# One layer on one core: the first double pair of gate and up as eight plain products instead of seven combined ones

## The chip, the core and the metric

The kernel runs on one core of a Trainium2 chip. The core has TensorE (PE, with its weight loads as PEld), VectorE (DVE), ScalarE (ACT), GpSimd (POOL) and a queue for transfers (SP). The metric is the device time of one execution in microseconds (us), the median over runs. Each engine works through its own list of instructions in a fixed order; a scheduler decides that order when the program is built.

## The reference, cut to what matters

The program is one transformer layer: a mixer, a cross attention and a SwiGLU block, each with a norm ahead and a norm behind. The change lies where the cross attention ends and the SwiGLU block begins:

```
x = x + rms_norm(cross_attention, xattn_norm_post)
h = rms_norm(x, ffn_norm_pre)            # 512 tokens x 1024
g, u = split(h @ w_gate_up)              # 2 x 2816 columns
y = (silu(g) * u) @ w_down
x = x + rms_norm(y, ffn_norm_post)
```

## The kernel before, in words

**Split floats.** Every operand of a product is held as two parts, hi and lo: `split` lets ACT write hi (L167) and DVE or POOL subtract it from the source to get lo (L168). A product of two operands is three matmuls, wl with hi, wh with lo, wh with hi (L1226 to L1228 for gate and up).

**Gate and up.** The 2 x 2816 columns are worked in eleven double pairs, d = 0 to 10, each of 256 columns of gate and 256 of up. In `gate_up(d)` the tokens are two halves (0 to 255, 256 to 511) and the 1024 rows of the weight are two halves (lo, hi), so h is four blocks 11, 12, 21, 22 (token half, row half). Gate and up of one double pair would be eight products of blocks. The kernel takes seven, in Winograd's form: 11, 12, S2, S1, S3, S4, 22 in that order, where S1 = 21 + 22, S2 = S1 - 11, S3 = 11 - 21, S4 = 12 - S2 are sums of token blocks, and the weights of those products are sums too (`t1`, and sums written over `ulo`, `glo`, `ghi`). A product is 24 matmuls of 256 columns.

**Where the blocks come from.** `dense_R` ends the cross attention, one token tile of 128 after another (bk_dR). Behind each tile `ev_second2` adds to the residual and calls `prenorm`, which norms the tile, transposes it on PE (bk_pn, L254) and hands it to `Blocks.store`. For tiles 0 and 1 that writes blocks 11 and 12 (A) as hi and lo; for all four tiles ACT also copies the plain numbers to a buffer `hr` (L1167). `Blocks.sums` (tiles 2 and 3, L1172 to L1178) builds S1 to S4 and 22 from the `hr` buffers with sums on DVE and POOL, and splits each of them.

**Order.** `steps` begins d = 0 and d = 1 with their product 11, then runs d = 0, then d = 1 and so on. The weights of d = 0 are in `fraw[0]` and those of d = 1 in `fraw[1]`, both loaded early: `fraw[1]` lies on the left, where the pool `tp` of the attention was.

**Down.** Behind the last double pair, `w_down` is split and multiplied (bk_ff). Weights there come from `fw[1]`, the split gate (`gs`) from `fw[0]`, four buffers each.

Of the kernel before, what the change touches and what calls it, by code (L numbers as in the profile page):

```python
# [14 lines left out]
P = 128  # L15
# [31 lines left out]
def hybrid_layer(ctx, tc, a, out):  # L47
# [13 lines left out]
    tp = late.enter_context(tc.tile_pool(name="tp", bufs=4))  # L61
    yp = late.enter_context(tc.tile_pool(name="yp", bufs=16))
    gp = late.enter_context(tc.tile_pool(name="gp", bufs=16))
    BUFS = {"sc": 3, "tr": 2, "pv": 1, "d": 2}
# [127 lines left out]
    class Big:  # L192
# [922 lines left out]
    fraw, fw, fn, fa, fg = ([pool("fr0", 2, "right")], [pool("fw0", 4, "right")], pool("fn", 2, "right"),  # L1115
                            [pool("fa0", 2, "right")], [pool("fg0", 5, "right")])
    count = [0]

    def wpair(shape=(P, 4, 256), half=None):

        if half is None:
            half = count[0] % 2
            count[0] += 1
        return [fw[half].tile(list(shape), F32R, tag="wc", name="w" + q) for q in "hl"]
# [16 lines left out]
    class Blocks:  # L1141

        def __init__(self):
            self.c, self.raw = {}, {}

        def take(self, pool, *names):
            for n in names:
                self.c[n] = pool.tile([P, 2, 4, 256], F32R, tag="A", name="A" + n)

        def put(self, n, i, src, eng=None):  # L1150
            c = slice(128 * (i % 2), 128 * (i % 2) + 128)
            t = self.c[n]
            split(t[:, 0, :, c], t[:, 1, :, c], src, eng)

        def hi(self, n, k):
            return self.c[n][:, 0, k, :]

        def lo(self, n, k):
            return self.c[n][:, 1, k, :]
# [34 lines left out]
    fw.append(pool("fw1", 4))
    fa.append(pool("fa1", 5))
    fg.append(pool("fg1", NF // 2 - 5))
    fe, ft = pool("fe", 6), pool("ft", 1)
    A.take(fa[1], "S2", "S1", "S3", "S4", "22")
    for i in range(2, NT):
        with tc.high_priority(offset=PLAN["fprio"]):  # L1200
            A.sums(i)

    Gf = {}

    def gate_up(d):

        raw = []
        for u in range(2):
            raw.append(fraw[d % 2].tile([P, KT, 256], F32, tag="raw", name="raw"))
            nc.sync.dma_start(raw[u], kview(w_gu)[:, :, FF * u + 256 * d:FF * u + 256 * d + 256])  # L1210
        g, u = raw
        glo, ghi, ulo, uhi = g[:, 0:4], g[:, 4:8], u[:, 0:4], u[:, 4:8]

        def weights(src, eng=None, half=None):
            w = wpair(half=half)
            split(*w, src, eng)
            return w

        def product(b, w, n, start):
            wh, wl = w  # L1220
            for z in range(2):
                c = slice(128 * z, 128 * z + 128)
                o = b[:, 256 * z:256 * z + 256]
                for k in range(4):
                    st = start and z == 0 and k == 0
                    nc.tensor.matmul(o, lhsT=wl[:, k, c], rhs=A.hi(n, k), start=st, stop=False, skip_group_check=True)  # L1226
                    nc.tensor.matmul(o, lhsT=wh[:, k, c], rhs=A.lo(n, k), start=False, stop=False, skip_group_check=True)  # L1227
                    nc.tensor.matmul(o, lhsT=wh[:, k, c], rhs=A.hi(n, k), start=False, stop=k == 3, skip_group_check=True)  # L1228

        def halves(t):  # L1230
            return t.rearrange("p (z t) -> p z t", z=2)
# [18 lines left out]
        yield  # L1250
# [18 lines left out]
        yield  # L1269
# [13 lines left out]
    for g in range(NF // 2):  # L1283
        raw = fraw[1 - g // 2 % 2].tile([P, 2, D], F32, tag="raw", name="raw")
        nc.sync.dma_start(raw, wd[:, 2 * g:2 * g + 2, :])
        for q in range(2):
            k = 2 * g + q
            if k >= NF - LAST:
                t = len(tail)
                gs = fw[t // 4].tile([P, 2, 512], F32R, tag="wc", name="gs")  # L1290
                w2 = fa[t >= 2].tile([P, 2, D], F32R, tag="A", name="wd")
                hi, lo = w2[:, 0, :], w2[:, 1, :]
            else:
                gs = fw[0].tile([P, 2, 512], F32R, tag="wc", name="gs")
                hi, lo = wpair((P, D), 1)
# [50 lines left out]
```

## Time and profile before

| | |
|---|---|
| median of 3 runs | 870.31 us (869.36 to 871.18) |
| the profiled execution | 870.79 us, its span 869.0 us |
| PE busy | 821.9 us, 95% of the span |
| DVE, ACT, POOL busy | 546.9, 431.9, 342.2 us |

PE is the engine that the others feed, so what counts is where it stands still or runs at its lower clock. The 40 slices of the page show that in one place in the middle of the program, in the 24th and 25th slice (a slice is 21.7 us).

### The profile page before, as it was taken

The numbers are of one execution on the slowest core, as the hardware profiler recorded it, in microseconds if no ns is written. First come the engines' busy times: TensorE is split into PE (matmuls) and PEld (weight loads), VectorE is DVE, ScalarE is ACT, GpSimd is POOL, SyncE is SP. The second block draws the span as 40 slices with busy tenths as digits, with TensorE's granted clock in tenths as the row PEclk, the third lists the DMA queues.
The fourth block names the chain that finished last, engine by engine and source line by source line (L and its number), as shares of the span: only waits on it lengthen the run. The fifth ranks groups of instructions, "written<-read, shape, count | busy, mean of one in ns | idle before, by whom it ended". The sixth has DMA issues, their size and how long they took to land.

```text
span 869.0 us, 12630 instructions
## 1 busy us (share of the span) xinstructions
PE 821.9 (95%) x4809; PEld 703.6 (81%) x4809; DVE 546.9 (63%) x913; ACT 431.9 (50%) x848; POOL 342.2 (39%) x246
## 2 busy tenths in 40 slices
PE   5899998998999999999999868999999999999997
PEld 3787667885688978778888668999999999888885
DVE  3528688687889835743553699888888775223313
ACT  5413566667867644634543654445544444224411
POOL 3405133255537443502311474644444454432320
PEclk9999999999999999999999988999999999999999
DMA  8633331321203331242226003333333333222101
GB/s 270 210 107 114 90 84 62 127 80 49 74 2 98 122 122 49 97 146 97 97 98 194 0 25 97 98 97 97 110 119 119 111 122 103 97 97 98 49 25 72
DMA packets 68307, 85.27 MB, mean 98 GB/s; under 512 B 4400, under 2 KB 53905, under 8 KB 68246
## 3 DMA queue, kind: packets, MB, share of 16 engines
q1 hardware_dynamic: 64574, 77.97, 27.7%
q10 hardware_dynamic: 3672, 6.50, 2.1%
q8 instruction: 38, 0.62, 0.3%
q14 instruction: 23, 0.19, 0.1%
HBM read 82.34 MB, written 2.12 MB: 97 GB/s over the span
## 4 chain that ended last, share of the span: by engine, by line
PE 75%; DVE 12%; ACT 6%; DMA 2%; issue 2%; POOL 1%; SPq 1%; ACTq 0%; DVEq 0%; POOLq 0%
PE bk_X L1226 5%; PE bk_X L1227 5%; PE bk_X L1228 5%; PE bk_ff L286 5%; PE bk_ff L287 5%; PE bk_ff L288 5%; PE bk_dT L286 4%; PE bk_dT L287 4%; PE bk_dT L288 4%; PE bk_pv L922 3%; PE bk_dN L287 3%; PE bk_dN L288 3%; PE bk_dN L286 3%; PE bk_Z L1226 2%; PE bk_Z L1227 2%; PE bk_Z L1228 2%
## 5 line engine op out<-in xcount | busy, mean ns | idle before, releaser
L167 ACT ACTIVATE wh<-raw 128x1024 fp32r<-128x1024 f32 x82 | 86.6, 1057 | 111.5 <-PE bk_ff L287 46.8
L168 DVE TENSOR_TENSOR wl<-raw,wh 128x1024 fp32r<-128x1024 f32 x60 | 86.2, 1439 | 60.1 <-ACT wh L167 60.1
L168 POOL TENSOR_TENSOR wl<-raw,wh 128x1024 fp32r<-128x1024 f32 x22 | 62.8, 2854 | 106.7 <-ACT wh L167 106.7
L167 ACT ACTIVATE whi<-raw 128x1024 fp32r<-128x1024 f32 (+1 forms) x64 | 60.0, 947 | 67.7 <-PE bk_dT L286 31.9
L168 POOL TENSOR_TENSOR wlo<-raw,whi 128x1024 fp32r<-128x1024 f32 x23 | 56.1, 2439 | 93.7 <-ACT whi L167 88.4
L286 PE MATMUL bk_dT<-hTh,wlo 128*128 128x512 f32 x192 | 76.9, 401 | 1.8 <-DVE wlo L168 1.1
L288 PE MATMUL bk_dT<-hTh,whi 128*128 128x512 f32 x192 | 76.6, 399 | 0.0
L287 PE MATMUL bk_dT<-hTl,whi 128*128 128x512 f32 x192 | 76.4, 398 | 0.0
L168 POOL TENSOR_TENSOR gs<-gf,gs 128x512 fp32r<-128x512 f32 x22 | 36.0, 1640 | 66.2 <-ACT gs L167 66.2
L1226 PE MATMUL bk_Z<-AS,wl 128*128 128x256 f32 x176 | 50.6, 287 | 6.6 <-DVE wl L168 6.6
L1226 PE MATMUL bk_X<-AS,wl 128*128 128x256 f32 x176 | 50.3, 286 | 3.7 <-ACT u L1249 3.7
L1226 PE MATMUL bk_X<-A,wl 128*128 128x256 f32 x176 | 50.3, 286 | 2.4 <-ACT A L167 1.3
L168 DVE TENSOR_TENSOR wlo<-raw,whi 128x1024 fp32r<-128x1024 f32 x25 | 32.7, 1313 | 31.5 <-ACT whi L167 31.3
L1227 PE MATMUL bk_Z<-AS,wh 128*128 128x256 f32 x176 | 50.6, 288 | 0.8 <-DVE AS L168 0.8
L288 PE MATMUL bk_ff<-wh,gs 128*128 128x512 f32 x128 | 50.8, 397 | 0.0
L287 PE MATMUL bk_ff<-wl,gs 128*128 128x512 f32 x128 | 50.7, 396 | 0.0
L1227 PE MATMUL bk_X<-A,wh 128*128 128x256 f32 x176 | 50.4, 287 | 0.2 <-DVE A L168 0.2
L1228 PE MATMUL bk_Z<-AS,wh 128*128 128x256 f32 x176 | 50.3, 286 | 0.0
L1228 PE MATMUL bk_X<-A,wh 128*128 128x256 f32 x176 | 50.1, 285 | 0.0
L1227 PE MATMUL bk_X<-AS,wh 128*128 128x256 f32 x176 | 49.6, 282 | 0.2 <-DVE AS L168 0.2
L1228 PE MATMUL bk_X<-AS,wh 128*128 128x256 f32 x176 | 49.5, 281 | 0.0
L892 POOL TENSOR_SCALAR s<-s,acf 128x128 f32<-128x128 f32 (+3 forms) x32 | 36.3, 1144 | 25.6 <-PE bk_tr L907 15.9
(372 smaller groups left out, 2543.4 us busy)
## 6 DMA issues: line engine op xcount, KB each, us to landing
raw<-in_w_gate_up_dram SPq DMA_DIRECT2D x22, 1024.0 KB, 7.4
raw<-in_w_down_dram SPq DMA_DIRECT2D x11, 1024.0 KB, 4.9
raw<-in_w_xkv_dram SPq DMA_DIRECT2D x8, 1024.0 KB, 5.1
raw<-in_w_in_dram SPq DMA_DIRECT2D x7, 1024.0 KB, 6.1
raw<-in_w_out_dram SPq DMA_DIRECT2D x4, 1024.0 KB, 5.1
raw<-in_w_xq_dram SPq DMA_DIRECT2D x4, 1024.0 KB
raw<-in_w_xo_dram SPq DMA_DIRECT2D x4, 1024.0 KB, 5.0
raw<-in_w_in_dram SPq DMA_DIRECT2D x6, 512.0 KB, 4.1
```

Source lines behind the costliest of these rows:

```text
L167: nc.scalar.activation(hi, src, AF.Copy)
L168: (eng or nc.vector).tensor_tensor(lo, src, hi.bitcast(F32), op=OP.subtract)
L286: nc.tensor.matmul(o, lhsT=wl, rhs=xh, start=start, stop=False)
L287: nc.tensor.matmul(o, lhsT=wh, rhs=xl, start=False, stop=False)
L288: nc.tensor.matmul(o, lhsT=wh, rhs=xh, start=False, stop=stop)
L892: ENG[on].tensor_scalar(s[:, 0:n], s[:, 0:n], c, None, op0=OP.mult)
L922: nc.tensor.matmul(o, lhsT=v, rhs=pTs[br][q][:, j], start=(br, j, q) == mms[0], stop=(br, j, q) == mms[-1])
L1226: nc.tensor.matmul(o, lhsT=wl[:, k, c], rhs=A.hi(n, k), start=st, stop=False, skip_group_check=True)
L1227: nc.tensor.matmul(o, lhsT=wh[:, k, c], rhs=A.lo(n, k), start=False, stop=False, skip_group_check=True)
L1228: nc.tensor.matmul(o, lhsT=wh[:, k, c], rhs=A.hi(n, k), start=False, stop=k == 3, skip_group_check=True)
```

## The change

- Double pair 0 is computed plainly, ahead of all sums: for each token half t, gate is 11 and 12 (or 21 and 22) with the weights' two row halves, added up in one bank, and up likewise in another. That is eight products, and neither sums of tokens nor of weights are needed for it.
- Its four weights (`w_first`) are loaded and split ahead of `dense_R` in the code.
- `store` writes all four blocks 11, 12, 21, 22 as hi and lo straight from the transposes; the `hr` copies are gone. Block 21 lies in four buffers of the pool `fe`, which moves to the right.
- `sums` comes behind the plain double pair, and gets its plain numbers back by adding hi and lo (`whole`: blocks 11 and 12 on POOL, 21 and 22 on DVE). All other sums and all their lo parts are on DVE now.
- The pool `tp` moves to the right side. `fraw[1]` now lies where the cross attention's input Ox was. `fw` is one ring of eight buffers, also for `w_down` and `gs`.
- The interleaved start of d = 0 and d = 1 is gone; d = 1 to 10 run as before, one behind the other.

```diff
+    fw = pool("fw", 8, "right")
+    fa = [pool("fa0", 3, "right")]
+    fe = pool("fe", 6, "right")
...
         def store(self, g, c0, c1, src):
             i = c0 // 128
-            if g == 0:
-                self.raw[i] = gtile(0, (P, 2, 4, 128), name="hr")
-            if i < 2:
-                self.put("12" if g else "11", i, src)
-            nc.scalar.activation(self.raw[i][:, g], src, AF.Copy)
+            self.put("%d%d" % (i // 2 + 1, g + 1), i, src)
...
         def sums(self, i):
...
+            q, r, s = (gtile((P, 2, 4, 128), name=n) for n in ("aq", "ar", "as"))
+            for n in range(2):
+                self.whole(q[:, n], "1%d" % (n + 1), i, nc.gpsimd)
+                self.whole(r[:, n], "2%d" % (n + 1), i, nc.vector)
+            nc.vector.tensor_tensor(s[:, 0], r[:, 0], r[:, 1], op=OP.add)
+            nc.vector.tensor_tensor(s[:, 1], s[:, 0], q[:, 0], op=OP.subtract)
+            self.put("S2", i, s[:, 1])
+            self.put("S1", i, s[:, 0])
+            nc.vector.tensor_tensor(r[:, 0], q[:, 0], r[:, 0], op=OP.subtract)
+            self.put("S3", i, r[:, 0])
+            nc.vector.tensor_tensor(q[:, 1], q[:, 1], s[:, 1], op=OP.subtract)
             self.put("S4", i, q[:, 1])
-            self.put("22", i, r[:, 1], nc.gpsimd)
...
+    w_first = [weights(q) for q in load_gu(0)]
...
-    for i in range(2, NT):
-        with tc.high_priority(offset=PLAN["fprio"]):
-            A.sums(i)
...
-    steps = [gate_up(d) for d in range(NF // 2)]
-    for d in (0, 0, 1, 1):
-        next(steps[d])
-    for t in steps:
-        run(t)
+    Gf[0] = gtile()
+    for t in range(2):
+        gate, up = bank("sc", "bk_X"), bank("d", "bk_Y")
+        for b, w in ((gate, w_first[0:2]), (up, w_first[2:4])):
+            for h in range(2):
+                product(b, w[h], "%d%d" % (t + 1, h + 1), h == 0, h == 1)
+        s1 = etile(name="s1")
+        nc.scalar.activation(s1, gate, AF.Silu)
+        nc.vector.tensor_tensor(Gf[0][:, :, 256 * t:256 * t + 256], halves(s1), halves(up), op=OP.mult)
+    for i in range(2, NT):
+        A.sums(i)
+    for d in range(1, NF // 2):
+        gate_up(d)
```

**ACT, where dense_R ends.** The first rows are of before, from the statistics of the last tile (pn) on; wh are hi parts of weights (raw), A11 and A12 the token blocks, xn the norm.

```order
L259 ACTIVATE pn_5025,ss1_5026<-bk_dR_4999 128x512
L167 ACTIVATE wh_5189<-raw_5183 128x1024
L167 ACTIVATE A11_4811<-bk_pn_4920 128x4x128
L247 ACTIVATE xn_4976<-x1_3426,rs_r_4980 128x512 x2
L167 ACTIVATE A12_4812<-bk_pn_4931 128x4x128
L167 ACTIVATE wh_5219<-raw_5183 128x1024
L242 ACTIVATE xn_5036,ss_5035<-x1_3426 128x1024
```

The same place after the change:

```order
L258 ACTIVATE pn_5048,ss1_5049<-bk_dR_5022 128x512
L166 ACTIVATE A11_4812<-bk_pn_4943 128x4x128
L246 ACTIVATE xn_4996<-x1_3426,rs_r_5000 128x512 x2
L166 ACTIVATE A12_4813<-bk_pn_4952 128x4x128
L241 ACTIVATE xn_5059,ss_5058<-x1_3426 128x1024
```

The two splits of weights of d = 1 are gone from between the blocks; the four of d = 0 all stand ahead of the first tile's pn.

**DVE, the sums.** Before, the sums and their lo parts (AS) begin right behind the last norm, mixed with weights (wl) of d = 0:

```order
L1172 TENSOR_TENSOR s1_5083<-hr_4989 128x512
L1173 TENSOR_TENSOR s2_5084<-s1_5083,hr_4862 128x512
L1172 TENSOR_TENSOR s1_5099<-hr_5048 128x512
L168 TENSOR_TENSOR AS2_5078<-s2_5084,AS2_5078 128x4x128
L1173 TENSOR_TENSOR s2_5100<-s1_5099,hr_4925 128x512
L168 TENSOR_TENSOR AS1_5079<-s1_5083,AS1_5079 128x4x128
L168 TENSOR_TENSOR wl_5285<-t1_5155,wh_5284 128x1024
```

After the change 27 instructions stand from the first output of the plain pair (gf, ahead of the sums) to the weight of d = 1's product S2 (wl_5415); these are the last ten of them, the second output among them:

```order
L167 TENSOR_TENSOR AS3_5099<-ar_5305,AS3_5099 128x4x128
L1257 TENSOR_TENSOR raw_5344<-raw_5345,raw_5344 128x1024
L167 TENSOR_TENSOR AS1_5098<-as_5326,AS1_5098 128x4x128
L1199 TENSOR_TENSOR aq_5324<-aq_5324,as_5326 128x512
L167 TENSOR_TENSOR AS4_5100<-aq_5304,AS4_5100 128x4x128
L167 TENSOR_TENSOR AS2_5097<-as_5326,AS2_5097 128x4x128
L1288 TENSOR_TENSOR gf_5101<-s1_5301,bk_Y_5204 128x2x256
L167 TENSOR_TENSOR AS3_5099<-ar_5325,AS3_5099 128x4x128
L1268 TENSOR_TENSOR raw_5344<-raw_5344 128x1024
L167 TENSOR_TENSOR wl_5415<-raw_5344,wh_5414 128x1024
```

The second half of S2 and the weight that goes with it now stand at the end of this chain, behind parts of S1, S3 and S4.

**SP, the loads of gate and up.** After the change (raw_4819 and raw_4820 are d = 0, raw_5344 and raw_5345 d = 1, raw_5567 and raw_5568 d = 2):

```order
L1221 DMA raw_4819<-in_w_gate_up_dram 128x8x256
L1221 DMA raw_4820<-in_w_gate_up_dram 128x8x256
L1221 DMA raw_5567<-in_w_gate_up_dram 128x8x256
L1221 DMA raw_5568<-in_w_gate_up_dram 128x8x256
L1221 DMA raw_5344<-in_w_gate_up_dram 128x8x256
L1221 DMA raw_5345<-in_w_gate_up_dram 128x8x256
```

The loads of d = 2 have moved ahead of those of d = 1, which now wait for PE's last use of Ox.

## Rows read from the trace of the kernel before

**Rows 1.** Busy time by stage; clock granted to PE, share of DMA, GB/s last
```profile
494.80:500.40 5.60, 1.81 (x10) 0.98 (x7) 4.85 (x6) 5.60 (x10) 4.25 (x5) 0.99 0.00 0
500.40:503.60 3.20, 3.08 (x14) 3.08 (x15) 3.20 (x5) 1.23 (x3) 3.20 (x2) 0.50 0.00 0
...
515.00:521.60 6.60, 0.05 (x1) 0.00 (x0) 6.60 (x6) 5.14 (x9) 5.97 (x4) 0.68 0.00 0
...
523.20:528.00 4.80, 4.74 (x23) 4.71 (x23) 4.80 (x5) 2.69 (x4) 4.61 (x3) 0.54 0.00 0
```

**Rows 2.** PE's waits from 494 to 735 us: total, times, longest
```profile
PE bk_Z L1226 <- DVE wl L168: 6.6, 1, 6.6
```

**Rows 3.** Timeline of PE: start, us, then what; in brackets the idle time before
```profile
494.43 1.03 PE L254 MATMUL bk_pn<-cc,xn 128*128 128x128 f32 x8
496.80 0.39 PE L1226 MATMUL bk_X<-A,wl 128*128 128x256 f32 x1 [1.34 <-ACT A L167]
...
505.96 0.60 PE L254 MATMUL bk_pn<-cc,xn 128*128 128x128 f32 x4
506.32 0.36 PE L1227 MATMUL bk_Y<-A,wh 128*128 128x256 f32 x1
...
521.67 0.55 PE L1226 MATMUL bk_Z<-AS,wl 128*128 128x256 f32 x1 [6.62 <-DVE wl L168]
...
523.64 0.41 PE L1228 MATMUL bk_Z<-AS,wh 128*128 128x256 f32 x1
523.85 0.41 PE L1226 MATMUL bk_Z<-AS,wl 128*128 128x256 f32 x1
...
532.89 0.35 PE L1226 MATMUL bk_X<-AS,wl 128*128 128x256 f32 x1 [1.49 <-ACT u L1249]
...
552.85 0.28 PE L1226 MATMUL bk_X<-A,wl 128*128 128x256 f32 x1
...
558.59 0.28 PE L1226 MATMUL bk_Y<-A,wl 128*128 128x256 f32 x1
```

**Rows 4.** Timeline of DVE
```profile
510.90 2.77 DVE L1173 TENSOR_TENSOR s<-s,hr 128x512 f32<-128x512 f32 x1
...
515.29 1.75 DVE L168 TENSOR_TENSOR AS<-s,AS 128x512 fp32r<-128x512 f32 x1
...
518.64 0.68 DVE L168 TENSOR_TENSOR AS<-s,AS 128x512 fp32r<-128x512 f32 x1
519.24 2.28 DVE L168 TENSOR_TENSOR wl<-t,wh 128x1024 fp32r<-128x1024 f32 x1
...
535.16 1.21 DVE L168 TENSOR_TENSOR wl<-raw,wh 128x1024 fp32r<-128x1024 f32 x1
536.30 0.67 DVE L1258 TENSOR_TENSOR p<-p,bk_X 128x512 f32<-128x512 f32 x1
...
569.64 1.23 DVE L1241 TENSOR_TENSOR raw<-raw 128x1024 f32<-128x1024 f32 x1
...
590.10 1.23 DVE L1241 TENSOR_TENSOR raw<-raw 128x1024 f32<-128x1024 f32 x1
```

**Rows 5.** Timeline of POOL
```profile
510.69 2.43 POOL L168 TENSOR_TENSOR wl<-raw,wh 128x1024 fp32r<-128x1024 f32 x1 [4.88 <-ACT wh L167]
```

**Rows 6.** Timeline of ACT
```profile
472.49 2.00 ACT L167 ACTIVATE wh<-raw 128x1024 fp32r<-128x1024 f32 x2
477.38 0.60 ACT L259 ACTIVATE pn<-bk_dR 128x512 f32<-128x512 f32 x1 [2.90 <-PE bk_dR L288]
...
494.63 0.60 ACT L259 ACTIVATE pn<-bk_dR 128x512 f32<-128x512 f32 x1
...
495.21 1.05 ACT L167 ACTIVATE wh<-raw 128x1024 fp32r<-128x1024 f32 x1
496.16 0.59 ACT L167 ACTIVATE A<-bk_pn 128x512 fp32r<-128x512 f32 x1
```

**Rows 7.** The tile raw, loads of gate and up from 440 to 560 us
```profile
DMA to landing us min/median/max: 7.6/8.1/10.0
```

More of the change, by code (lines that the diff above doesn't have):

```diff
@@ L60, in hybrid_layer @@
     sl = early.enter_context(tc.tile_pool(name="sl", bufs=6, side="right"))
-    tp = late.enter_context(tc.tile_pool(name="tp", bufs=4))
+    tp = early.enter_context(tc.tile_pool(name="tp", bufs=4, side="right"))
     yp = late.enter_context(tc.tile_pool(name="yp", bufs=16))
@@ L113, in hybrid_layer @@
         "cprio": 600,
-        "fprio": 800,
         "mprio": 100,
@@ L1114, in hybrid_layer, with wtile, weights @@
     early.close()
[L1115 to L1124, printed above, removed]
+    fraw = [pool("fr0", 2, "right")]
+    fw = pool("fw", 8, "right")
+    fn = pool("fn", 2, "right")
+    fa = [pool("fa0", 3, "right")]
+    fe = pool("fe", 6, "right")
+    def wtile(shape=(P, 4, 256), name="wc"):
+        return fw.tile(list(shape), F32R, tag="wc", name=name)
+    def weights(src, eng=None):
+        w = wtile(name="wh"), wtile(name="wl")
+        split(*w, src, eng)
+        return w
     def etile(shape=(P, 512), name="e"):
@@ L1133, in ntile, with gtile @@
         return fn.tile(shape, F32, tag="xn", name=name, bufs=2)
-    def gtile(half, shape=(P, 2, 512), name="gf"):
-        return fg[half].tile(list(shape), F32, tag="gf", name=name)
+    def gtile(shape=(P, 2, 512), name="gf"):
+        return fg.tile(list(shape), F32, tag="gf", name=name)
     class Blocks:
         def __init__(self):
-            self.c, self.raw = {}, {}
+            self.c = {}
         def take(self, pool, *names):
@@ L1148, in take, with piece, hi, lo @@
                 self.c[n] = pool.tile([P, 2, 4, 256], F32R, tag="A", name="A" + n)
+        def piece(self, n, q, k):
+            if n == "21":
+                return self.c[n][q][k // 2]
+            return self.c[n][:, q, k:k + 2, :]
+        def hi(self, n, k):
+            return self.piece(n, 0, k // 2 * 2)[:, k % 2, :]
+        def lo(self, n, k):
+            return self.piece(n, 1, k // 2 * 2)[:, k % 2, :]
         def put(self, n, i, src, eng=None):
             c = slice(128 * (i % 2), 128 * (i % 2) + 128)
-            t = self.c[n]
@@ L1153, in put @@
[L1153 to L1159, printed above, removed]
+            if n == "21":
+                for k in (0, 2):
+                    split(self.piece(n, 0, k)[:, :, c], self.piece(n, 1, k)[:, :, c], src[:, k:k + 2], eng)
+            else:
+                t = self.c[n]
+                split(t[:, 0, :, c], t[:, 1, :, c], src, eng)
         def store(self, g, c0, c1, src):
@@ new lines, in whole @@
+        def whole(self, o, n, i, eng):
+            c = slice(128 * (i % 2), 128 * (i % 2) + 128)
+            if n == "21":
+                for k in (0, 2):
+                    h, l = (self.piece(n, q, k)[:, :, c].bitcast(F32) for q in range(2))
+                    eng.tensor_tensor(o[:, k:k + 2], h, l, op=OP.add)
+            else:
+                h, l = (self.c[n][:, q, :, c].bitcast(F32) for q in range(2))
+                eng.tensor_tensor(o, h, l, op=OP.add)
+        def sums(self, i):
+            q, r, s = (gtile((P, 2, 4, 128), name=n) for n in ("aq", "ar", "as"))
[9 more added lines that the diff above has]
+            nc.vector.tensor_tensor(q[:, 1], q[:, 1], s[:, 1], op=OP.subtract)
+            self.put("S4", i, q[:, 1])
@@ new lines, in product @@
+    def product(b, w, n, start, stop=True):
+        wh, wl = w
+        for z in range(2):
+            c = slice(128 * z, 128 * z + 128)
+            o = b[:, 256 * z:256 * z + 256]
+            for k in range(4):
+                st = start and z == 0 and k == 0
+                nc.tensor.matmul(o, lhsT=wl[:, k, c], rhs=A.hi(n, k), start=st, stop=False, skip_group_check=True)
+                nc.tensor.matmul(o, lhsT=wh[:, k, c], rhs=A.lo(n, k), start=False, stop=False, skip_group_check=True)
+                nc.tensor.matmul(o, lhsT=wh[:, k, c], rhs=A.hi(n, k), start=False, stop=stop and k == 3,
+                                 skip_group_check=True)
@@ L1182, in hybrid_layer, with halves, load_gu @@
+    def halves(t):
+        return t.rearrange("p (z t) -> p z t", z=2)
+    def load_gu(d):
+        raw = [fraw[d % 2].tile([P, KT, 256], F32, tag="raw", name="raw") for _ in range(2)]
+        for u in range(2):
+            nc.sync.dma_start(raw[u], kview(w_gu)[:, :, FF * u + 256 * d:FF * u + 256 * d + 256])
+        return [raw[u][:, 4 * h:4 * h + 4] for u in range(2) for h in range(2)]
     w_gu = a["w_gate_up"][0]
@@ L1184, in hybrid_layer @@
     A = Blocks()
-    A.take(fa[0], "11", "12")
+    A.take(fa[0], "11", "12", "22")
+    A.c["21"] = [[fe.tile([P, 2, 256], F32R, tag="e", name="A21") for _ in range(2)] for _ in range(2)]
+    w_first = [weights(q) for q in load_gu(0)]
     def ev_second2(i, b):
@@ L1193, in hybrid_layer @@
     fraw.append(pool("fr1", 2))
[L1194 to L1198, printed above, removed]
-    for i in range(2, NT):
-        with tc.high_priority(offset=PLAN["fprio"]):
-            A.sums(i)
+    fa.append(pool("fa1", 4))
+    fg = pool("fg", NF // 2)
+    ft = pool("ft", 1)
+    A.take(fa[1], "S2", "S1", "S3", "S4")
     Gf = {}
     def gate_up(d):
[L1207 to L1231, printed above, removed]
+        glo, ghi, ulo, uhi = load_gu(d)
         X, Y = bank("sc", "bk_X"), bank("d", "bk_Y")
-        product(X, weights(glo, half=d if d < 2 else None), "11", True)
+        product(X, weights(glo), "11", True)
         x1 = etile(name="x1")
         nc.scalar.activation(x1, X, AF.Copy)
-        w21 = weights(ghi, nc.gpsimd, d if d < 2 else None)
+        w21 = weights(ghi, nc.gpsimd)
         t1 = ft.tile([P, 4, 256], F32, tag="t1", name="t1")
@@ L1287, in hybrid_layer @@
             k = 2 * g + q
+            gs = wtile((P, 2, 512), name="gs")
             if k >= NF - LAST:
-                t = len(tail)
-                gs = fw[t // 4].tile([P, 2, 512], F32R, tag="wc", name="gs")
-                w2 = fa[t >= 2].tile([P, 2, D], F32R, tag="A", name="wd")
+                w2 = fa[len(tail) >= 3].tile([P, 2, D], F32R, tag="A", name="wd")
                 hi, lo = w2[:, 0, :], w2[:, 1, :]
             else:
-                gs = fw[0].tile([P, 2, 512], F32R, tag="wc", name="gs")
-                hi, lo = wpair((P, D), 1)
+                hi, lo = wtile((P, D), name="whi"), wtile((P, D), name="wlo")
             split(gs[:, 0], gs[:, 1], Gf[g][:, q], nc.gpsimd)
```

18 lines of the change are left out of this document (1 added, 17 removed).

## The prediction

> **What bounds the kernel now.** I read the page first: PE is busy for 95% of the span, so the time is PE's, and a gain must come from where PE stands still or is clocked down. The windows by stage put that place right behind `dense_R` [rows 1]: from 494.8 to 500.4 PE works 1.81 of 5.6 us, then 3.2 us at a granted clock of 0.50, then it stands still from 515.0 to 521.6, and from 523.2 to 528.0 it is back at 0.54. The list of waits names the worst single one, 6.6 us, once, for a lo part of a weight on DVE [rows 2]. In those windows DVE and, mostly, POOL are busy almost without a break, so PE waits for the sums of tokens and for the weights that stand among them in DVE's order.
>
> How much that costs is read from PE's timeline [rows 3]. The last transposes that PE issues ahead of gate and up begin at 494.43 and take about 0.6 us to issue, so PE is free at about 495.05. At the other end bk_X holds the product 22 of d = 1 and then 11 of d = 2, from 552.85 to 558.59: 5.74 us for 48 matmuls, 0.1196 us each, so d = 2 begins at 552.85 + 2.87 = 555.7. Between 495.05 and 555.7 lie 60.65 us, for 14 products, or 336 matmuls, that need 40.2 us. With 16 transposes (four cost 0.36 us, from 505.96 to 506.32, so 1.44 in all) some 19 us are lost. The slow clock is in that: matmuls start 0.21 us apart at 523.64, 0.09 more than at full clock.
>
> **The change, step by step.** I lay PE's new sequence along the same time axis.
>
> Ahead of gate and up. Two more weights of d = 0 are split before the first tile's pn. ACT takes 2.00 us for two from 472.49 and waits 2.90 us before 477.38 [rows 6], so two more hide in that gap; only some 0.9 us of it is left. DVE does four lo parts instead of one, 1.13 apart, and ends just past 478; the cover is the rest of `dense_R`, 16 us of PE work. Without that cover, a late first tile would be late again at every norm behind it. I cost it at nothing.
>
> The start. Before, ACT splits a weight of d = 1 at 495.21 and only then, at 496.16, block 11 of tile 1 [rows 6], for which PE waits until 496.80 [rows 3]. In the new order that split is gone, so the block comes 0.95 earlier and PE starts at 495.85. The second matmul needs the lo part, one 0.68 subtraction [rows 4] with a handover, so PE runs from about 496.65: 1.6 us idle. A wait of 1.49 at 532.89 left the matmul at 0.35 us, not 0.55 as behind the wait of 6.62 [rows 3]; I count no clock loss here.
>
> The plain pair. Eight products, 192 matmuls at 0.1196, are 22.96, with the 1.44 of transposes: token half 0 ends at 496.65 + 11.48 + 1.44 = 509.6, token half 1 at 521.05. The extra product alone is 2.87 of it. Blocks 21 and 22 must be there at 509.6. Their lo parts read the banks of the transposes, which are issued by 507; the last of them follows by my count at about 509.3, with 0.3 us to spare for the first piece and 1.8 for the last, since its matmul comes 13 later.
>
> Double pair 1 then has 11 and 12 first (5.74, to 526.8) and needs S2 at 526.8. A whole pair in the steady part takes 590.10 - 569.64 = 20.46 us [rows 4]. With no further wait d = 1 would end at 521.05 + 20.46 = 541.5 instead of 555.7. **That is 14.2 us less, if the sums stay hidden.**
>
> The sums. DVE can begin when up of token half 0 is complete, at 509.6 and a handover, 509.9. From there to the weight of S2 stand 27 instructions: 19 of 512 elements, 4 of 256, 4 of 1024. Uncontended they follow each other at 0.60 (518.64 to 519.24) and 1.14 (535.16 to 536.30) [rows 4]; for 256 elements no row exists, between nothing and 0.60, and I take 0.35. That is 11.4 + 1.4 + 4.6 = 17.4, so 527.3: just 0.5 us late. But POOL slows DVE. While POOL runs, 512 elements take 1.75 instead of 0.68 and 1024 take 2.28 instead of 1.21, and the sum at 510.90, caught under POOL's 2.43 us from 510.69, takes 2.77 [rows 4, 5]. Two lo parts of d = 1's weights (those of ghi and of ulo) come to POOL within the chain by ACT's order, at about 517 and 528. If each holds up two instructions of DVE by 1.07, that is 4.3 us, and S2 starts at 531.6: PE waits 4.8. The Trainium skill ("SBUF — State Buffer", on the two sides of SBUF) states that the port pair which VectorE and GpSimd share is an exclusive lock for a whole instruction, so that the loser fully blocks; by that, twice 2.43 makes 4.9 instead of 4.3, and S2 0.6 later, and the 2.77 above, which ends 0.55 after POOL's instruction, agrees. A wait of this size is nearer to the 6.62 than to the 1.49, so I count the slow clock behind it: some 20 matmuls at 0.09 more (23 ran in the slow stretch from 523.2 to 528.0), 1.8. **Together 6.6 us are given back.** Bounds: 0.5 with no contention and no slow clock; 11 if the four `whole` sums on POOL (each 512 elements) also hold up DVE ahead of 509.6 by 1.07 each and so move the whole chain.
>
> What costs nothing. The `hr` copies on ACT and POOL's eight sums and splits go away (four `whole` sums come), off PE's path as soon as nothing waits for them. From S1 on the weights are back ahead of PE: after S2, DVE needs 1.14 for the next lo part and PE 2.87 per product. In `w_down` three buffers per row block come from one ring of eight, so a lo part waits for the row block two earlier; a block is 24 matmuls of twice the columns, so 2 x 2.87 = 5.7 us on PE, and the lo part 1.21 on DVE, so it is covered by some 4 us a block, and 16 blocks would pay if that cover were gone. The loads of d = 2 now start behind the first splits of weights, by my count near 476, far ahead of need. Behind SP's waiting loads of d = 1 stand only those of d = 3 and later.
>
> The sum: 870.31 - 14.2 + 6.6 = 862.7; I say 862.6. The profiled execution took 870.79, 0.48 above the median; the stage that I price lies in its span, and I subtract the difference from the median.
>
> **The rivals.**
> *The sums stay hidden* (0.20). If ACT hands POOL its weights a few instructions later or earlier, the contention falls on DVE instructions that read a bank, such as the 0.67 at 536.30, or behind the chain. Then PE waits under 2 us and the clock holds: 856 to 859. For it: POOL has far less in this stretch than before (5.97 of 6.6 us busy in the wait window). Against it: uncontended the chain is already as long as its cover.
> *The chain starts late* (0.15). The four `whole` sums on POOL meet the norm of tile 3 and two weight sums on DVE; blocks 21 and 22 come after 509.6, PE waits there, and everything behind shifts: 4 us more, 865 to 868.5.
> *Slower* (0.05). DVE's order has `t1` of d = 1 between two pieces of block 21, and it needs both loads of d = 1, which now wait for the last use of Ox. If they are issued near 491, and land 7.6 to 10.0 us later [rows 7], they are there at 501, ahead of need, which by my count of DVE's norms is at about 504. But if Ox is only released when `dense_R` has ended and the loads come behind d = 2's, each us past 506 delays blocks 21 and 22 and with them PE. From a landing at about 514 on, 8 us late with the 6.6 above, the whole 14.2 is gone; at 520 it would be 876. Nothing in the rows shows a load near twice 10 us.
> The rest of my chance (0.60) is for the forecast, 860 to 865.
>
> **How the numbers follow.** A measurement of this kernel tells about 0.2%, 1.7 us, from no change: faster means under 868.6, slower over 872. Forecast, hidden sums and nearly all of the late chain are faster: 0.92. A late chain with a further wait of 2 to 3 us would end near 870: 0.03 for the same. Slower has 0.05. The range reaches from the middle of the hidden case, 857, to the upper part of the late chain, 867; below and above lie about 2 in 10.
>
> **What would show it.** In the profile after: PE's first long row of A products from 496 to 497; no clock under 1.00 until about 527; bk_Y's product for the second token half ended at about 521; then one wait of 3 to 6 us on the first S2 matmul, for DVE's wl, and a stretch of some 4 us at about 0.50 behind it; d = 2 beginning at 548 instead of 555.7; 20.46 per pair from there, and the same span from bk_ff on. I am wrong if the wait is missing, if it lies ahead of the second token half, if DVE waits for the load of d = 1, or if PE waits in `w_down`, where it did not before.

## The result, and the profile after

The changed kernel takes 864.37 us (median of 4 runs, 862.70 to 864.66) beside 870.25 us for the kernel before on the same chip: a ratio of 0.9928, 95% interval 0.9911 to 0.9946, so 0.7% faster; the medians lie 5.9 us apart. The profiled execution took 864.1 us, its span 862.3, which is 6.7 less than the span before.

PE's waits from 485 to 735 us of the kernel after (waited for, total us, times, longest) are these; they answer to [rows 2].

```profile
engine line waited for: us in total, times, longest us
PE bk_X L1210 <- ACT u L1263: 2.4, 8, 0.6
PE bk_pn L253 <- DVE A L167: 2.0, 1, 2.0
PE bk_X L1210 <- DVE wl L167: 2.0, 1, 2.0
PE bk_Y L1210 <- POOL wl L167: 2.0, 1, 2.0
```

The one wait of 6.6 has become three of 2.0. PE's timeline has them in order of time (start, us, then the operation; in brackets the idle time ahead of it and what ended it); it answers to [rows 3].

```profile
496.63 0.39 PE L1210 MATMUL bk_X<-A,wl 128*128 128x256 f32 x1 [0.54 <-ACT A L166]
...
509.01 0.63 PE L253 MATMUL bk_pn<-cc,xn 128*128 128x128 f32 x4 [2.02 <-DVE A L167]
...
530.83 0.39 PE L1210 MATMUL bk_Y<-A,wl 128*128 128x256 f32 x1 [1.96 <-POOL wl L167]
...
535.99 0.36 PE L1210 MATMUL bk_X<-AS,wl 128*128 128x256 f32 x1 [2.01 <-DVE wl L167]
```

The windows of the same stage (columns as in [rows 1]) show the slow clock behind the first and the last of them: 0.50 from 510 to 513, 0.64 from 536 to 540.

```profile
507.00:509.00 2.00, 0.00 (x0) 0.02 (x1) 2.00 (x3) 1.97 (x4) 2.00 (x2) 1.00 0.42 136
...
510.00:513.00 3.00, 3.00 (x16) 3.00 (x15) 2.10 (x4) 1.04 (x3) 0.00 (x0) 0.50 0.00 0
...
526.00:532.00 6.00, 4.04 (x33) 3.83 (x33) 6.00 (x8) 4.07 (x5) 6.00 (x2) 1.00 0.00 0
532.00:536.00 4.00, 1.99 (x18) 1.81 (x16) 4.00 (x3) 1.06 (x1) 1.62 (x1) 1.00 0.00 0
536.00:540.00 4.00, 4.00 (x23) 4.00 (x24) 4.00 (x5) 0.63 (x1) 0.00 (x0) 0.64 0.00 0
```

What DVE did meanwhile, from its timeline after:

```profile
497.33 3.47 DVE L282 SCALAR_TENSOR_TENSOR x<-yo,rs_r,x 128x512 f32<-128x512 f32 x2
...
502.83 3.48 DVE L249 SCALAR_TENSOR_TENSOR xn<-x,rs_r,gain 128x512 f32<-128x512 f32 x2 [0.66 <-POOL rs_r L235]
506.23 0.41 DVE L167 TENSOR_TENSOR A<-bk_pn,A 128x256 fp32r<-128x256 f32 x1
506.56 1.97 DVE L1255 TENSOR_TENSOR t<-raw 128x1024 f32<-128x1024 f32 x1
508.45 1.01 DVE L167 TENSOR_TENSOR A<-bk_pn,A 128x256 fp32r<-128x256 f32 x2
...
514.51 0.69 DVE L1288 TENSOR_TENSOR gf<-s,bk_Y 128x512 f32<-128x512 f32 x1 [2.39 <-PE bk_Y L1212]
...
527.88 0.68 DVE L167 TENSOR_TENSOR AS<-as,AS 128x512 fp32r<-128x512 f32 x1
528.49 0.68 DVE L1288 TENSOR_TENSOR gf<-s,bk_Y 128x512 f32<-128x512 f32 x1
529.08 2.25 DVE L167 TENSOR_TENSOR AS<-ar,AS 128x512 fp32r<-128x512 f32 x1
531.26 3.45 DVE L1268 TENSOR_TENSOR raw<-raw 128x1024 f32<-128x1024 f32 x1
534.62 1.22 DVE L167 TENSOR_TENSOR wl<-raw,wh 128x1024 fp32r<-128x1024 f32 x1
```

And POOL's timeline:

```profile
502.76 6.90 POOL L1186 TENSOR_TENSOR aq<-A 128x512 f32<-128x512 f32 x4
521.89 11.72 POOL L167 TENSOR_TENSOR wl<-raw,wh 128x1024 fp32r<-128x1024 f32 x2 [12.23 <-ACT wh L166]
```

The two lo parts apart, from the view of the tile wl from 500 to 545 us (ns shortest/median/longest, first and last start):

```profile
L167 POOL TENSOR_TENSOR wl<-raw,wh x2: 2870/5878/8887, 521.9 to 530.7; 128x1024 fp32r<-128x1024 f32 x2
```

Read together: from 515 to 528.5 DVE is not slowed at all. Its sums start 0.60 apart and last 0.68, so the next begins before the last has ended. POOL's lo part of ghi, which needs 2.43 us [rows 5], starts at 521.89 and ends 8.89 later, at 530.78. It gets through when DVE runs an instruction that takes one input from a bank, the memory that PE writes its sums to (gf, 528.49). PE waits for that lo part until 530.83. Then DVE stands behind POOL, twice: 2.25 instead of 0.68, and 3.45 instead of 1.22. So in this chain POOL was the loser first, and PE waited for both. That isn't so in every chain of sums: in the kernel before, POOL had begun first, and then it and DVE took turns through such sums, one instruction each (512 elements in 1.75 on DVE [rows 4]; on POOL these):

```profile
513.08 1.74 POOL L1176 TENSOR_TENSOR hr<-hr 128x512 f32<-128x512 f32 x1
514.78 1.72 POOL L1178 TENSOR_TENSOR hr<-hr,s 128x512 f32<-128x512 f32 x1
```

d = 2 begins at 551.85 (bk_X holds 22 and 11 from 548.97, half of its 48 matmuls are 2.87). From PE's release at 495.68 that is 56.17 us, against 60.65 before: the stage gave 4.5 us. PE enters it 0.63 later than before (495.05). The missing 3 us lie in `w_down`. Two windows, of matmuls on bk_ff alone, first the kernel before:

```profile
760.00:830.00 70.00, 70.00 (x301) 56.26 (x300) 0.00 (x0) 0.00 (x0) 1.00 0.22 76
```

and after:

```profile
760.00:830.00 70.00, 70.00 (x310) 57.90 (x309) 0.00 (x0) 0.00 (x0) 1.00 0.21 75
```

In the same 70 us, with PE busy throughout and the full clock in both, 310 matmuls start instead of 301. Over all 528 the mean distance from one start to the next is 227.8 ns instead of 233.5, 3.0 us in all. (After the change one gap of 3.1 us is left out of this: the last 24 matmuls of gate and up run in it.) So 4.5 + 3.0 - 0.63 = 6.9, near the 6.7 of the spans.

### The profile page after: what moved, and what is told of

Its sections match the earlier page's. It is cut to its first block, busy times and chain, and to the rows that moved or that the text cites. A ratio compares the mean times of both kernels' runs of the same rounds, so it can differ in the third digit from the quotient of the medians.

```text
span 862.3 us, 12664 instructions
## 1 busy us (share of the span) xinstructions
PE 822.5 (95%) x4833; PEld 707.7 (82%) x4833; DVE 543.1 (63%) x925; ACT 424.3 (49%) x838; POOL 326.9 (38%) x238
## 5 line engine op out<-in xcount | busy, mean ns | idle before, releaser
L166 ACT ACTIVATE whi<-raw 128x1024 fp32r<-128x1024 f32 (+1 forms) x80 | 76.8, 967 | 69.6 <-PE bk_dT L285 31.9
L167 DVE TENSOR_TENSOR wlo<-raw,whi 128x1024 fp32r<-128x1024 f32 x41 | 55.0, 1343 | 80.1 <-PE bk_ff L286 43.0
L166 ACT ACTIVATE wh<-raw 128x1024 fp32r<-128x1024 f32 x64 | 67.3, 1057 | 60.6 <-PE bk_X L1210 24.5
L167 DVE TENSOR_TENSOR wl<-raw,wh 128x1024 fp32r<-128x1024 f32 x44 | 63.3, 1444 | 10.3 <-ACT wh L166 10.3
L1211 PE MATMUL bk_X<-A,wh 128*128 128x256 f32 x192 | 54.4, 283 | 0.3 <-DVE A L167 0.3
L1212 PE MATMUL bk_X<-A,wh 128*128 128x256 f32 x192 | 54.2, 283 | 0.0
L286 PE MATMUL bk_ff<-wlo,gs 128*128 128x512 f32 x128 | 49.8, 389 | 0.0
L287 PE MATMUL bk_ff<-whi,gs 128*128 128x512 f32 x128 | 49.6, 389 | 0.0
L285 PE MATMUL bk_ff<-whi,gs 128*128 128x512 f32 x128 | 47.4, 389 | 0.0
L1212 PE MATMUL bk_X<-AS,wh 128*128 128x256 f32 x160 | 45.6, 285 | 0.0
L1211 PE MATMUL bk_X<-AS,wh 128*128 128x256 f32 x160 | 45.5, 285 | 0.0
L285 PEld LDWEIGHTS bk_dT<-hTh,wlo 128*128 128x128 f32 x192 | 36.3, 189 | 10.8 <-DVE wlo L167 1.9
L1210 PE MATMUL bk_Z<-AS,wl 128*128 128x256 f32 x160 | 45.0, 281 | 0.0
```

What stands on the lines that cost most here:

```text
L166: nc.scalar.activation(hi, src, AF.Copy)
L167: (eng or nc.vector).tensor_tensor(lo, src, hi.bitcast(F32), op=OP.subtract)
L285: nc.tensor.matmul(o, lhsT=wl, rhs=xh, start=start, stop=False)
L286: nc.tensor.matmul(o, lhsT=wh, rhs=xl, start=False, stop=False)
L287: nc.tensor.matmul(o, lhsT=wh, rhs=xh, start=False, stop=stop)
```

## The experiments

The theory was: what is still lost behind `dense_R` is DVE and POOL holding each other up around the sums, and the 3 us come from where `w_down`'s buffers lie. Its rivals: the sums are simply too long for DVE, and the order of `w_down`'s products makes its pace. In the table, each ratio is to runs of the kernel before on the same chip, "stage" is worked out as from PE's first product of gate and up to the start of d = 2, and "bk_ff" is that mean distance.

| kernel | median us | ratio to before (95%) | stage us | bk_ff ns |
|---|---|---|---|---|
| before | 870.25 | | 58.9 | 233.5 |
| after the change | 864.37 | 0.9911 to 0.9946 | 55.2 | 227.8 |
| e1, no sums | 855.5 | 0.9814 to 0.9845 | 45.6 | 227.8 |
| e2, lo parts of d = 1 on DVE | 857.0 | 0.9827 to 0.9853 | 49.9 | 227.8 |
| e6, e2 and later whole sums | 856.31 | 0.9798 to 0.9842 | 47.4 | 227.8 |
| e7, later whole sums alone | 861.46 | 0.9865 to 0.9903 | 52.7 | 227.8 |
| e9, e6 and blocks moved by 32 bytes | 856.1 | 0.9781 to 0.9843 | 47.3 | 228.6 |
| e3, before with a ring in `w_down` | 869.91 | 0.9987 to 1.0005 | 59.3 | 231.9 |
| e4, before with sides swapped | 869.78 | 0.9965 to 0.9992 | 59.1 | 233.2 |
| e5, before with `fw1` on the right | 870.61 | 0.9982 to 1.0008 | 62.4 | 228.2 |
| e8, before with weights 32 bytes later | 869.78 | 0.9966 to 1.0000 | 59.6 | 231.7 |
| e10, before with sums on DVE alone | 870.5 | 0.9971 to 1.0008 | 58.0 | 233.5 |

**e1: no sums at all.**

```diff
-    A.take(fa[1], "S2", "S1", "S3", "S4")
+    A.c.update(S2=A.c["12"], S1=A.c["22"], S3=A.c["11"], S4=A.c["12"])
...
-    for i in range(2, NT):
-        A.sums(i)
```

> The changed kernel without any sums of tokens: S1 to S4 are stood in for by finished blocks, so DVE's chain and POOL's four whole sums are gone; all products and sums of weights stay. If the sums, and the two engines' contention over them, are what the plain pair still pays for, the waits on bk_Y (2.0, for POOL's wl) and on S2 (2.0, for DVE's wl) and the slow clock behind S2 (about 1.3) vanish: about 859 us, d = 2 beginning near 546.5 instead of 551.85. The wait of 2.0 on bk_pn should shrink, not vanish, since the norm of tile 3 stays: 0.5 to 2 more, so 857 to 859.5. If instead the waits come from DVE's sums of weights and splits alone, it stays at 862.5 to 864.5.

Measured 855.5 us, under the range. All three waits of 2.0 are gone, and the clock is 1.00 from 495 to 545. The first wait vanished too, which I had expected only in part. DVE's timeline says why:

```profile
503.17 1.42 DVE L249 SCALAR_TENSOR_TENSOR xn<-x,rs_r,gain 128x512 f32<-128x512 f32 x2 [0.66 <-POOL rs_r L235]
504.50 0.42 DVE L167 TENSOR_TENSOR A<-bk_pn,A 128x256 fp32r<-128x256 f32 x1
504.84 1.21 DVE L1255 TENSOR_TENSOR t<-raw 128x1024 f32<-128x1024 f32 x1
```

With no whole sums on POOL, tile 3's norm takes 1.42 instead of 3.48 and `t1` 1.21 instead of 1.97: together 2.8 us less in front of the block of tile 2 for which PE waited 2.0. So of the 55.2 us of the stage, 9.6 hang on the sums, in one way or another.

**e2: the two lo parts of d = 1 on DVE.**

```diff
-        w21 = weights(ghi, nc.gpsimd)
+        w21 = weights(ghi, nc.vector if d == 1 else nc.gpsimd)
...
-        product(X, weights(ulo, nc.gpsimd), "S3", False)
+        product(X, weights(ulo, nc.vector if d == 1 else nc.gpsimd), "S3", False)
```

> The changed kernel with the two lo parts of d = 1 that POOL makes (ghi, ulo) on DVE instead. If POOL being locked out is the cost, the wait on bk_Y (2.0) goes, DVE no longer stands behind POOL (AS at 2.25 and a sum of weights at 3.45 instead of 0.6 and 1.2, so 3.9 less, against 1.2 more for the added lo part), S2 comes some 2.7 earlier and needs no wait, and the clock holds there: 859 to 860.5 us. If the mere length of DVE's chain sets S2, the added 1.2 shows: 864.5 to 866.

Measured 857.0 us, under the range: DVE does more, and the kernel is faster still. PE's waits now:

```profile
PE bk_pn L253 <- DVE A L167: 2.0, 1, 2.0
...
PE bk_X L1210 <- DVE wl L167: 0.4, 1, 0.4
```

The waits on bk_Y and (but for 0.4) on S2 are gone. DVE runs without a break from 514.60, and the same two instructions that took 2.25 and 3.45 take:

```profile
526.17 1.22 DVE L167 TENSOR_TENSOR wl<-raw,wh 128x1024 fp32r<-128x1024 f32 x1
...
530.31 0.68 DVE L167 TENSOR_TENSOR AS<-ar,AS 128x512 fp32r<-128x512 f32 x1
530.91 1.22 DVE L167 TENSOR_TENSOR wl<-raw,wh 128x1024 fp32r<-128x1024 f32 x1
532.05 1.22 DVE L1268 TENSOR_TENSOR raw<-raw 128x1024 f32<-128x1024 f32 x1
```

The stage is 5.3 us shorter than after the change: 2.0 on bk_Y, 1.6 on S2 and some 1.2 of slow clock are 4.8 of that. The built order moved a little with the edit: an added lo part (526.17) now stands ahead of S2's weight (530.91), and the sum of weights at 532.05 behind it, so DVE has as much to do before S2 as after the change. From gf to S2 it takes 17.7 us (514.60 to 532.28) instead of 21.5 (514.51 to 535.99). So it was not the length of DVE's chain alone that PE waited for, but POOL's place in it. (The medians differ by 7.4; the spans, 862.3 and 856.4, by 5.9.)

**e6 and e7: the whole sums on POOL later,** with e2's edit and without it. The sums' target now takes the buffers of the norms xn, so that they can't begin ahead of the transposes.

```diff
-            q, r, s = (gtile((P, 2, 4, 128), name=n) for n in ("aq", "ar", "as"))
+            q = ntile((P, 2, 4, 128), name="aq")
+            r, s = (gtile((P, 2, 4, 128), name=n) for n in ("ar", "as"))
```

> As the run with d = 1's lo parts on DVE (857.0), and POOL's four whole sums take the buffers of the norms xn of tiles 2 and 3, so that they can't begin ahead of the transposes of those tiles (some 505.5 and 507 to 510 instead of 502.9). If POOL's whole sums beside DVE's norm of tile 3 make the wait of 2.0 on bk_pn, DVE's xn x2 falls from 3.47 to about 1.4, the wait and the slow clock behind it (0.66 from 509 to 514, some 1.6) go: 853 to 854.5 us, about the level without any sums (855.5) or under it. If DVE's own t1 and sum of weights between the block reads make that wait, it stays: 856.5 to 857.5.

> The changed kernel with the whole sums on POOL held back in the same way, and d = 1's lo parts still on POOL. If the first wait is from the whole sums, it goes (2.0 and about 1.6 of slow clock), while the lock-out of POOL's lo part and the waits on bk_Y and S2 stay, because PE then asks for them as early as it comes: some 1 to 3.5 less than the changed kernel, 861 to 863.5 us. If the waits behind it simply grow by what is won ahead (DVE's chain is bound to the end of token half 0, so it moves along, but POOL's lo part hangs on ACT), it stays at 864.

e6 measured 856.31 us, between its two ranges, though its stage is 2.5 us shorter than e2's. The time can't tell the two ranges apart: its interval is 3.8 us wide, and the profiled execution came to its first product 1.3 later than e2's (498.04 against 496.74), with the same code ahead. So the answer is read from the stage. Half the wait is left: `PE bk_pn` 1.0. The rows of e6 on DVE and POOL:

```profile
504.24 2.45 DVE L249 SCALAR_TENSOR_TENSOR xn<-x,rs_r,gain 128x512 f32<-128x512 f32 x2 [0.66 <-POOL rs_r L235]
...
504.34 3.51 POOL L1186 TENSOR_TENSOR aq<-A 128x512 f32<-128x512 f32 x2
```

I had put tile 2's two sums at 505.5; they started at 504.34, still beside the norm, which takes 2.45, between the 3.48 of after and the 1.42 of e1, and beside `t1`, which still takes 1.98. With a wait of 1.0 the clock holds: 1.00 from 509 to 514, where e2 has 0.66.

```profile
509.00:514.00 5.00, 4.59 (x39) 4.62 (x40) 3.90 (x8) 2.30 (x5) 2.68 (x2) 1.00 0.06 18
```

e7 measured 861.46 us, 2.9 less than after and inside its range. The first wait halves, where I had it go; the two behind stay within 0.02 us.

```profile
508.16 0.63 PE L253 MATMUL bk_pn<-cc,xn 128*128 128x128 f32 x4 [1.02 <-DVE A L167]
528.48 0.39 PE L1211 MATMUL bk_Y<-A,wl 128*128 128x256 f32 x1 [1.97 <-POOL wl L167]
533.60 0.36 PE L1211 MATMUL bk_X<-AS,wl 128*128 128x256 f32 x1 [1.99 <-DVE wl L167]
...
519.52 11.71 POOL L167 TENSOR_TENSOR wl<-raw,wh 128x1024 fp32r<-128x1024 f32 x2 [7.36 <-ACT wh L166]
```

POOL's two lo parts take 11.71, after the change 11.72: the lock-out repeats, and it is independent of the first wait. The two edits add up: 2.5 us of stage each way for the first, 5.3 for the second.

**e10: is the plain pair needed, if POOL is the trouble?** The kernel before, with its share of POOL at the start on DVE.

```diff
-            nc.gpsimd.tensor_tensor(r[:, 0], q[:, 0], r[:, 0], op=OP.subtract)
-            self.put("S3", i, r[:, 0], nc.gpsimd)
-            nc.gpsimd.tensor_tensor(q[:, 1], q[:, 1], s2, op=OP.subtract)
+            nc.vector.tensor_tensor(r[:, 0], q[:, 0], r[:, 0], op=OP.subtract)
+            self.put("S3", i, r[:, 0])
+            nc.vector.tensor_tensor(q[:, 1], q[:, 1], s2, op=OP.subtract)
             self.put("S4", i, q[:, 1])
-            self.put("22", i, r[:, 1], nc.gpsimd)
+            self.put("22", i, r[:, 1])
...
-        w21 = weights(ghi, nc.gpsimd, d if d < 2 else None)
+        w21 = weights(ghi, nc.vector if d < 2 else nc.gpsimd, d if d < 2 else None)
...
-        product(X, weights(ulo, nc.gpsimd), "S3", False)
+        product(X, weights(ulo, nc.vector if d < 2 else nc.gpsimd), "S3", False)
```

> The kernel before, without the plain pair, but with POOL's share of the sums and lo parts at its start (S3, S4, 22, and ghi and ulo of d = 0 and 1) on DVE. If the two engines' contention alone made the wait of 6.6 and the plain pair is not needed, S1 is ready some 3 to 4 us earlier: 863 to 867 us. If the work ahead of the products is too long for one engine even undisturbed (by the built order 17 instructions from the first sum at 510 to the last part of S1, some 12 to 13 us, so near 522.5, where it stands now), the wait stays: 869 to 874 us.

Measured 870.5 us, no change. The wait of 6.6 splits into several, and from 516 to 522 PE works 1.07 of 6 us, with DVE busy for all of it, ACT for 5.96 and POOL for nothing (in the window PE, PEld, DVE, ACT):

```profile
PE bk_Z L1226 <- ACT AS L167: 2.7, 1, 2.7
PE bk_Z L1227 <- DVE AS L168: 2.3, 1, 2.3
PE bk_X L1226 <- DVE wl L168: 1.9, 2, 1.1
...
516.00:522.00 6.00, 1.07 (x2) 0.48 (x2) 6.00 (x9) 5.96 (x10) 0.00 (x0) 0.72 0.00 0
```

So contention alone did not make the wait. Without the plain pair the sums have no cover, and with POOL's share on it DVE, with ACT all but as full beside it, is too slow even undisturbed; with the plain pair (e2) DVE is fast enough. The plain pair and a quiet POOL are worth 14 us together (870.9 to 857.0, on one chip), the first alone 6, the second alone nothing; 3 us in the 14 and in the 6 are `w_down`'s.

**e3, e4, e5, e8: the pace of `w_down`.** All four are the kernel before with one thing of `w_down`'s buffers changed. In e3 `dtile` takes a buffer of `fw[0]` and of `fw[1]` in turn:

```diff
-                gs = fw[0].tile([P, 2, 512], F32R, tag="wc", name="gs")
-                hi, lo = wpair((P, D), 1)
+                gs = dtile((P, 2, 512), "gs")
+                hi, lo = dtile((P, D), "whi"), dtile((P, D), "wlo")
```

In e4 the two pools change places:

```diff
+                gs = fw[1].tile([P, 2, 512], F32R, tag="wc", name="gs")
+                hi, lo = wpair((P, D), 0)
```

In e5 both pools lie on the right, and `tp` too, which makes the room:

```diff
-    fraw, fw, fn, fa, fg = ([pool("fr0", 2, "right")], [pool("fw0", 4, "right")], pool("fn", 2, "right"),
+    fraw, fw, fn, fa, fg = ([pool("fr0", 2, "right")], [pool("fw0", 4, "right"), pool("fw1", 4, "right")], pool("fn", 2, "right"),
...
-    fw.append(pool("fw1", 4))
```

And in e8 the weights start 32 bytes further on:

```diff
-                hi, lo = wpair((P, D), 1)
+                hi, lo = (t[:, 8:8 + D] for t in wpair((P, D + 16), 1))
```

> The kernel before, with only the buffers of w_down changed: gs, whi and wlo take turns through the eight buffers of both sides instead of four for gs and four for weights. In the built order PE's products then stand as triples (wh with gs lo, wl with gs hi, wh with gs hi) as after the change, not five firsts ahead of five pairs. If the 3 us that w_down gained come from this, bk_ff matmuls start some 227.5 ns apart on average instead of 233.5, and the time is about 867.2 us. If the cadence came with something else of the change, it stays at 233.5 and 870.2 us.

> The kernel before, with the two sides swapped in w_down: gs on the left, its weights on the right; PE's order keeps its groups of five firsts ahead of five pairs. If the order of the products makes the cadence, it stays at about 233.5 ns and 870.2 us. If the place of the weights (on the right after the change) makes it, it falls to about 227.5 ns and the time to 867.2 us.

> The kernel before with only memory moved: fw1 (the weights of w_down) lies on the right beside fw0, at the addresses that the ring has after the change, and tp goes to the right to make room. PE's order in w_down keeps its five firsts ahead of five pairs. If the place makes the cadence, bk_ff matmuls come to about 227.8 ns on average and the time to about 867 us; if place and order are needed together, it stays near 232 to 233.5 ns and 869.5 to 870.5 us. The start of gate and up (the wait of 6.6) should not change by either.

> The kernel before with one thing changed: whi and wlo of w_down start 32 bytes further into their buffers, still on the left; gs on the right, the order of products and all else stay. Then the moving operand and the weights both start at 32 bytes modulo 64, as they do after the change; before, one starts at 0 and the other at 32. If that relation makes the cadence of bk_ff, it falls from 233.5 to about 228 ns on average, worth 2.5 to 3 us: about 868 us. If the side of the memory makes it, it stays at 233.5 and 871 us.

All four times lie within 0.3% of before, so the answer is read from the pace (e4's interval lies clear of 1 with its pace all but unchanged; why, I don't know). In e3 PE's order is that of after, and the pace is 231.9: the order isn't enough, though e3 moves operands from side to side too and so doesn't test the order by itself. In e4 sides are swapped, order kept: 233.2. In e5 both operands lie on the right, with the old order, so the new order isn't needed. The windows of e3, e4, e5 and e8 in turn; in e5 311 matmuls start in the 70 us:

```profile
760.00:830.00 70.00, 70.00 (x304) 56.64 (x303) 0.00 (x0) 0.00 (x0) 1.00 0.21 76
760.00:830.00 70.00, 70.00 (x302) 56.31 (x301) 0.00 (x0) 0.00 (x0) 1.00 0.21 76
760.00:830.00 70.00, 70.00 (x311) 57.94 (x310) 0.00 (x0) 0.00 (x0) 1.00 0.22 76
760.00:830.00 70.00, 70.00 (x304) 56.70 (x303) 0.00 (x0) 0.00 (x0) 1.00 0.20 76
```

So the place makes it, and 2.8 of the 3.0 us of the change are memory, not the plain pair. That e5 as a whole is no faster (870.61) is its start: with blocks elsewhere the built order moved there too, PE waits 5.3 and 4.4 us, and from the first product to bk_ff it takes 3.2 us more (245.9 against 242.7), which eats the 2.8 that `w_down` wins.

```profile
PE bk_Z L1225 <- ACT AS L167: 5.3, 1, 5.3
PE bk_Z L1226 <- DVE AS L168: 4.4, 1, 4.4
```

What it is about the place is only half settled. By the addresses in the built programs, the buffers of `w_down` on the right start at 32 bytes modulo 64, those on the left at 0. e8 moves the weights on the left by 32 bytes (and, with the longer buffers, the blocks S1 to S4 and 22 by 256, which leaves them where they were modulo 64): 231.7, a third of the way. So the relation of the two starts counts, but on different sides it doesn't bring the whole.

**e9: the same relation for 256 columns.** In the kernel after, products whose block and weight both start at 32 modulo 64 (11, 12, 21, 22) run 120 ns apart, those of S1 to S4, with the block at 0, 117.5 to 118.5: the other way round than in `w_down`. e9 is e6 with a gap of 32 bytes ahead of the right-hand blocks.

```diff
+    pool("gap", 1, "right").tile([P, 8], F32, tag="gap", name="gap")
     fa = [pool("fa0", 3, "right")]
```

> As the run with lo parts on DVE and later whole sums (856.3), with a gap of 32 bytes ahead of the blocks 11, 12, 22 and 21. Products of 256 columns start 120 ns apart where block and weight both start at 32 modulo 64, and 117.5 to 118.5 where the block starts at 0 (S1 to S4). If the relation of the two addresses makes that, the 888 or so matmuls of 11, 12, 21 and 22 come to about 118 too: 888 x 2 ns is 1.8 us less, while 72 matmuls of w_down (wd on the right) go from about 227 to 233 ns, 0.4 us more: 854.5 to 855.5 us. If the side makes it, they stay at 120 and the time at 856.3.

The matmuls moved as forecast: those of 11, 12, 21 and 22 to 118.3 ns (median 117, from 120), and the 72 of `w_down` whose weights lie in the same pool from 227.5 to 233.5. So there, on the right side alone, a shift of 32 bytes made the whole difference. The time didn't follow: 856.1 beside 856.3, intervals overlapping, and from the first product to the last of gate and up 232.8 us beside 233.1. I can't say where the rest of the 1.8 went; the waits for u grew from 2.0 to 2.6 and the one on S2 from 0.4 to 0.7.

## Why the prediction was right, and where it was not

The time, 862.6, lies 1.8 under the measured one and the range held it. But that is in part luck: two of its steps failed and offset each other. The stage gave 4.5 instead of 7.7, and `w_down` gave 3.0 that were not foreseen. By the stage alone the outcome is the rival "the chain starts late" (4 us more), and the cause is the one named there, POOL's whole sums beside the norm; only that PE waited for a bank and not yet for the blocks. Without the 3.0 us of `w_down` the time would have been some 867.4, an estimate, and over the range's upper end.

- *Ahead of gate and up, nothing:* right as far as it can be read. The entry is 0.63 later, but executions with the same code ahead differ by twice that (e2 and e6).
- *The start:* right in kind, 0.8 late. First product at 496.63, forecast 495.85; PE runs without a gap from 497.47, forecast 496.65. Of that 0.63 is the later entry. The clock stays at 1.00, as forecast.
- *Token half 0 ends at 509.6:* failed; bk_X for token half 1 begins at 514.3. I asked when the products would need blocks 21 and 22. The stall came ahead of that: tile 3's transposes need the bank that DVE has yet to read for tile 2, and they stand in PE's order ahead of half of up. PE waits 2.02 and loses some 1.5 to the clock (14 matmuls in 3.14 us from 510.08 to 513.22, where 1.68 would do). Of the other 1.2, 0.6 is the start (two matmuls had run ahead of 497.47); the rest I didn't follow. Its cause is the bound that I named and didn't take, the whole sums on POOL: e1, without them, has no such wait, and e7, which begins them later, has half of it. By my own signs, a wait ahead of the second token half, this step is wrong.
- *The sums:* the size was right, the order of winning and losing was not. From gf of token half 0 to S2 I forecast 21.7 us (509.9 to 531.6); it took 21.5 (514.51 to 535.99). Of DVE's 4.3 us behind POOL 3.8 came: (2.25 - 0.68) + (3.45 - 1.22). But I had POOL take its turn at each request, about 517 and 528. It was locked out for 8.89 us, came through at the end, and cost PE a wait of its own on bk_Y, for product 12 of d = 1, that I didn't have. The rule that I drew on, of the Trainium skill ("SBUF — State Buffer", on the two sides of SBUF), is that the pair is a lock for a whole instruction and the loser blocks. DVE's two rows behind POOL agree: the 2.25 ends 0.55 behind POOL's first lo part (530.78), the 3.45 1.1 behind its second (533.6). POOL's 8.89 fit only if DVE took the pair anew for each of its instructions, which no row shows by itself; which engine loses is what I got wrong.
- *6.6 us given back:* 1.96 and 2.01 of waits and about 1.2 of slow clock (23 matmuls from 536 to 540, 4.0 us instead of 2.8) are 5.2 behind token half 0, and 3.5 ahead of its end that I had at nothing. Instead of one wait of 3 to 6 us on S2 there were two of 2.0, and d = 2 begins at 551.85, not 548.
- *`w_down` costs nothing:* the waits stayed at none as argued, but the step was mis-sized by 3.0 us, a gain from where the ring lies (e5).
- *20.46 per pair from d = 2:* right; and the loads of d = 1 came in time, so the rival on the slower side had no ground.

## What to carry to other kernels

A helper engine beside a busy one is not a free hand: in one dense chain of sums POOL's 2.43 us became 8.89, and PE, which needed the result, waited with it. Near the bound, giving the busy engine more work and the helper none was worth 5.3 us of this stage, and e2's 857.0 us beats both kernels (e6's 856.3 is not told apart from it). When buffers are moved, compare the pace of the matmuls that read them, not only the waits; and when a block is due, ask not just when its product needs it but when the bank that it comes from is needed next.

## What the hardware showed that I had not expected

- POOL's instruction of 2.43 us took 8.89 us behind eleven DVE instructions that overlap (0.60 apart, 0.68 long), and again in e7 (11.71 for two), while beside the norms (3.48 for two of DVE, 6.90 for four of POOL) and in the sums of the kernel before (1.75 on DVE, 1.72 on POOL) the two took turns. Why they take turns in one place and not in the other no run here tells.
- A wait of 1.02 us left the clock at 1.00 behind it (e6, e7), one of 2.02 brought it to 0.66 over the next 5 us (e2). A wait of 1.96 at 530.83 left it at 1.00 until the next one, too.
- The pace of 512-column matmuls, with PE never waiting, is 227 or 232 to 234 ns by where the two operands lie (227.5 to 233.5 by a shift of 32 bytes alone, e9), and that of 256-column ones 117 to 120, by a shift of 32 bytes in the opposite sense.
